# Query, key and value sums of a decoder layer, taken two 128-token blocks at a time

## The chip, the core and the metric

The kernel runs on one core of a Trainium2 chip. A core has five engines with a queue each, and every queue works strictly in its own order: TensorE (PE in the profile; its weight loads are PEld), VectorE (DVE), ScalarE (ACT), GpSimd (POOL) and SyncE (SP), which here only issues DMA transfers. Engines wait for each other by semaphores. Matmul results land in PSUM, which this kernel divides into eight buffers of 128 x 512 float32.

The metric is the device time of one execution in microseconds (us), the median of several runs. A profiled execution gives the trace from which all rows below come; its span runs from the first to the last instruction.

## The reference, cut to what matters

The program is a two-layer decoder trunk on 512 tokens of width 1024. Layer 0 is a convolution module, layer 1 is causal differential attention; each is followed by a gated feed-forward network and a gated per-layer embedding. The change lies in layer 1:

```
u = rms_norm(h, g)                              # 512 x 1024
q, k, v = split(u @ w_qkv, 3)                   # 8 heads, 2 components of 64, v 128 wide
q = rms_norm(q, q_g) / 8;  k = rms_norm(k, k_g) # over each 64
for every block of 128 queries:
    logits = q_blk @ k.T + bias[bucket(distance)], masked to the past
    probs = softmax(logits)
    w = probs[component 0] - lam * probs[component 1]
    out = w @ v
h = h + (rms_norm(out, sub_g) * (1 - lambda_init)) @ w_o
```

Only `u @ w_qkv`, and the order in which parts of the block loop are put between its matmuls, are touched.

## The kernel before, in words

All products are in a split form: a float32 operand is held as a rounded part and its remainder (`hi`, `lo`), and one product is three matmuls (`mm3`, lines 154 to 156): hi by lo, lo by hi, hi by hi. A weight block of 128 x 1024 is loaded by SP into one of two `wraw` buffers, rounded by ACT (line 148), and its remainder is taken by DVE or, for chosen ones, by POOL (line 149); four such pairs can be held.

The activations `u` have the tokens along the free dimension, 8 row blocks of 128 features by 512 tokens. The six slabs of `w_qkv` (`QKV`, line 81) are each four weight blocks, that is eight row blocks of 128 x 512. A "q" slab holds the queries and keys of two heads (a pair), a "v" slab the values of four heads. For each slab and each of four token blocks `tokens` (line 634) sums over the eight row blocks: 24 matmuls of 128 x 128 by 128 x 512 into one buffer of the PSUM tag `mm`, which has four. So a slab is 96 matmuls, and the stage is 576.

What comes after a sum depends on the slab. `values` (650) scales and splits it into the tile `B` (ACT line 654, DVE line 655). `unit` (661) copies it (ACT 670), squares it (ACT 673), sums the squares (DVE 677), takes the power -1/2 on POOL (213) and scales it on POOL (680). `unit_end` (683) comes later: four transposes on TensorE (686) into one of two `tp` buffers, then ACT writes the rounded queries and keys (694, 695), POOL copies the keys to the other half (699), and DVE writes the four remainders (702, 704).

The attention of a head and a block of 128 queries is cut in three steps. `stage_s` makes the scores (TensorE 731, 732, into one of two `sc` buffers), adds the bias and finds the maximum on DVE (734), takes the exponential on ACT (738) and combines the two components on DVE (741 to 743). `stage_t` transposes the result (751), and ACT and DVE split it (753, 754). `stage_a` multiplies it with the values (767, 768); every second block ends with a read by ACT and DVE (774, 775), and the fourth block of a head with its norm (779 to 789). `stage_o` transposes a finished head (796) and splits it (168, 169) for the output product.

The steps stand in one list (line 803 on). The place n of a score step is 4 x head + block; the transpose of the same block stands at n + 2 and the product at n + 3, so from n = 3 to n = 31 there are three steps to every n. The loop over `QKV` (815) hands them out: `take(3 * pace)` gives each token block so many steps, and one is issued after each row block's three matmuls. The last place is for the `unit_end` of the block before. What is left after the six slabs is handed out between the matmuls of the per-layer embedding projection (844 on, three steps per output block) and of the output product (`linear`, 867).

The program's text does not fix the order on the engines: a planner with a model of the engines' times reorders the instructions within their dependencies, and its result is the order that is built. Each engine then keeps to that order.

## Time and profile before

| | us |
|---|---|
| median of 3 runs | 1321.56 |
| lowest and highest run | 1321.38, 1324.51 |
| the profiled execution | 1322.03 |
| its span | 1320.2 |
| TensorE busy | 1283.0 |
| DVE busy | 755.1 |
| ACT busy | 526.1 |
| POOL busy | 258.4 |

The stage of the six slabs lies between 652.3 and 816.5 us of the span, what is left of the attention runs to about 881 us beside the projection and the first output columns. A row of a group gives the line, the engine, the operation, the tiles (output, then inputs, without buffer numbers), the shapes and the count; behind the bar the busy time in us, the mean duration of one in ns, and the idle time of the engine ahead of them with what ended it. A row of the waits gives who waited for whom, the total in us, how often, and the longest. A row of the timeline gives the start, the duration, the engine and the line.

### The profile page before, as it was taken

What the parts mean: (1) busy time and instruction counts of PE and PEld (TensorE: products, weight loads), DVE (VectorE), ACT (ScalarE), POOL (GpSimd) and SP (SyncE); (2) the same over time, 40 slices, a digit from 0 to 9 for tenths busy, and PEclk for the clock granted to TensorE, in tenths of its full rate; (3) what the DMA queues carried; (4) which work ended last, traced back from release to release, by engine and by line L of the source; (5) the groups of instructions that cost most, each with busy time, mean ns of one, the idle gap of its engine ahead of it and who ended that gap; (6) DMA issues with size and microseconds to landing.
All of it is one profiled execution on the core that took longest, in us unless ns stands there. A gap on an engine that the chain in (4) does not pass through costs nothing. (4 is left out here: it accounts for less than half of the span.)

```text
span 1320.2 us, 15336 instructions
## 1 busy us (share of the span) xinstructions
PE 1283.0 (97%) x5852; PEld 1049.5 (79%) x5852; DVE 755.1 (57%) x1168; ACT 526.1 (40%) x830; POOL 258.4 (20%) x208
## 2 busy tenths in 40 slices
PE   8999889999999999999999998899999999999998
PEld 6777658888888888888888887778888888888887
DVE  6988684644344434455668887946543344334445
ACT  5644253422122222244466676734322222222342
POOL 5844342100000000022254544222000000000030
PEclk8999889999999999999999999999999999999999
DMA  6354412232322222233212321313223233332231
GB/s 218 110 170 155 132 33 94 82 97 98 104 98 98 97 96 96 80 104 102 87 65 83 102 73 41 103 34 126 96 96 96 96 97 99 102 97 93 76 123 65
DMA packets 45830, 129.21 MB, mean 98 GB/s; under 512 B 5267, under 2 KB 13587, under 8 KB 45756
## 3 DMA queue, kind: packets, MB, share of 16 engines
q1 hardware_dynamic: 39888, 122.70, 27.9%
q10 hardware_dynamic: 5868, 5.53, 1.3%
q8 instruction: 46, 0.75, 0.2%
q14 instruction: 28, 0.23, 0.1%
HBM read 124.52 MB, written 3.69 MB: 97 GB/s over the span
## 5 line engine op out<-in xcount | busy, mean ns | idle before, releaser
L148 ACT CAST whi<-wraw 128x1024 fp32r<-128x1024 f32 (+2 forms) x214 | 218.6, 1026 | 587.9 <-PE mm L156 367.8
L154 PE MATMUL mm<-A,wlo 128*128 128x512 f32 (+1 forms) x1096 | 426.0, 392 | 7.9 <-ACT A L492 3.8
L155 PE MATMUL mm<-A,whi 128*128 128x512 f32 (+1 forms) x1096 | 429.5, 393 | 1.4 <-DVE A L494 0.9
L156 PE MATMUL mm<-A,whi 128*128 128x512 f32 (+1 forms) x1096 | 426.9, 390 | 0.0
L149 DVE TENSOR_TENSOR wlo<-wraw,whi 128x1024 fp32r<-128x1024 f32 (+2 forms) x207 | 255.4, 1237 | 64.0 <-ACT whi L148 63.7
L154 PEld LDWEIGHTS mm<-A,wlo 128*128 128x128 f32 x1096 | 206.9, 189 | 54.7 <-ACT A L492 4.6
L155 PEld LDWEIGHTS mm<-A,whi 128*128 128x128 f32 x1096 | 207.0, 189 | 47.6 <-DVE A L169 3.2
L156 PEld LDWEIGHTS mm<-A,whi 128*128 128x128 f32 x1096 | 207.1, 189 | 43.5 <-issue 1.4
L188 POOL TENSOR_TENSOR acc<-acc,wk 128x512 f32<-128x512 f32 x42 | 68.6, 1632 | 781.8 <-issue 671.2
L155 PE MATMUL mm<-B,whi 128*128 128x512 f32 x352 | 136.9, 389 | 0.0
L156 PE MATMUL mm<-B,whi 128*128 128x512 f32 x352 | 136.9, 389 | 0.0
L154 PE MATMUL mm<-B,wlo 128*128 128x512 f32 x352 | 136.3, 389 | 0.0
L542 DVE TENSOR_TENSOR big<-mm,rb 128x512 f32<-128x512 f32 x44 | 30.4, 691 | 126.2 <-PE mm L156 126.2
L550 DVE TENSOR_TENSOR h<-mm,h 128x512 f32<-128x512 f32 x48 | 33.0, 691 | 120.7 <-PE mm L156 120.7
L540 DVE TENSOR_TENSOR big<-mm,rb 128x512 f32<-128x512 f32 x44 | 30.4, 691 | 99.3 <-PE mm L156 92.9
L154 PEld LDWEIGHTS mm<-B,wlo 128*128 128x128 f32 x352 | 66.1, 188 | 13.8
L156 PEld LDWEIGHTS mm<-B,whi 128*128 128x128 f32 x352 | 66.1, 188 | 13.7
L155 PEld LDWEIGHTS mm<-B,whi 128*128 128x128 f32 x352 | 66.1, 188 | 13.6
L156 PE MATMUL mm<-whi,A 128*128 128x512 f32 x192 | 75.7, 395 | 0.0
L155 PE MATMUL mm<-wlo,A 128*128 128x512 f32 x192 | 75.0, 396 | 0.0
L154 PE MATMUL mm<-whi,A 128*128 128x512 f32 x192 | 74.8, 396 | 0.0
L213 POOL TENSOR_TENSOR r<-v,mhalf 128x8 f32<-128x8 f32 (+1 forms) x31 | 47.5, 1532 | 121.7 <-DVE v L211 99.2
(193 smaller groups left out, 1426.1 us busy)
## 6 DMA issues: line engine op xcount, KB each, us to landing
wraw<-in_wts SPq DMA_DIRECT2D x194, 512.0 KB, 3.5
D<-in_diag SPq DMA_DIRECT2D x36, 192.0 KB, 3.9
wraw<-in_wts SPq DMA_DIRECT2D x16, 384.0 KB, 2.9
h<-in_xT SPq DMA_DIRECT2D x8, 256.0 KB, 5.3
bias<-scr ACTq DMA_DIRECT2D x8, 256.0 KB, 3.2
out_t<-h SPq DMA_DIRECT2D x7, 256.0 KB, 2.0
wraw<-in_wts SPq DMA_DIRECT2D x4, 256.0 KB, 3.4
wraw<-in_pT SPq DMA_DIRECT2D x4, 256.0 KB, 3.3
```

The source lines that it names most:

```text
L148: A.copy(hi[:, cut], raw[:, cut])
L149: eng.tensor_tensor(lo[:, cut], raw[:, cut], f(hi[:, cut]), ALU.subtract)
L154: T.matmul(acc, al, bh, start=first, stop=False)
L155: T.matmul(acc, ah, bl, start=False, stop=False)
L156: return T.matmul(acc, ah, bh, start=False, stop=last)
L188: self.eng.tensor_tensor(self.acc, self.acc, sq, ALU.add)
L213: last_pow[0] = G.tensor_tensor(r[:, :n], v[:, :n], mhalf[:, :n], ALU.pow)
L540: V.tensor_tensor(tg, pg, rb, ALU.mult)
L542: V.tensor_tensor(tu, pu, rb, ALU.mult)
L550: V.tensor_tensor(h[m], acc, h[m], ALU.add)
```

## The change

A slab's token blocks are now taken in two pairs. `tokens` opens two `mm` buffers and goes through the row blocks once for both, the second block one row block behind the first: three matmuls of the first block with row block n, then three of the second block with row block n - 1. After each such triple one place is free for a step, so a pair has 16 places.

`QKV` now carries two numbers per slab, one for each pair: `take(n)` hands out all steps whose place in the list is below that number. The last number is 21. The `unit_end` of the two blocks of the pair before stand at the 12th and the 14th of the 16 places (12 places are filled with steps or left empty, and the two are set in behind the 11th and at the end); those of the last pair follow behind the stage. `values` and `unit` get the finished sums and run one after the other at the end of a pair.

```diff
-QKV = (("q", 0, (0, 0, 0, 0)), ("v", 0, (0, 1, 1, 0)), ("q", 1, (1, 1, 2, 2)), ("q", 2, (0, 1, 2, 0)), ("v", 1, (1, 2, 2, 2)), ("q", 3, (0, 2, 0, 1)))
+QKV = (("q", 0, (0, 0)), ("v", 0, (2, 4)), ("q", 1, (6, 8)), ("q", 2, (9, 11)), ("v", 1, (14, 17)), ("q", 3, (19, 21)))
...
-    def tokens(ws, tb, between=()):
-        acc = mm()
-        for k in range(NC):
-            a = tuple(t[:, tb * P : (tb + 1) * P] for t in u[k])
-            mm3(acc, a, ws[k], k == 0, k == NC - 1)
-            if k < len(between) and between[k]:
-                between[k]()
+    def tokens(ws, tbs, between):
+
+        accs = [mm() for _ in tbs]
+        for n in range(NC + 1):
+            for acc, tb, k in ((accs[0], tbs[0], n), (accs[1], tbs[1], n - 1)):
+                if 0 <= k < NC:
+                    a = tuple(t[:, tb * P : (tb + 1) * P] for t in u[k])
+                    mm3(acc, a, ws[k], k == 0, k == NC - 1)
+                    if between:
+                        s = between.pop(0)
+                        if s:
+                            s()
...
     def take(n):
-        got, stages[:n] = [s for _, s in stages[:n]], []
+        got = [s for at, s in stages if at < n]
+        del stages[: len(got)]
         return got
 
-    waiting = None
+    waiting = []
     for what, at, pace in QKV:
         ws = slab(GLO if at > 0 else 0)
-        for tb in range(4):
-            between = take(3 * pace[tb])
-            between += [None] * (6 - len(between))
-            if waiting:
-                between.append(partial(unit_end, *waiting))
-                waiting = None
-            if what == "v":
-                values(at, ws, tb, between)
-            else:
-                waiting = unit(at, ws, tb, between)
-    unit_end(*waiting)
+        for i in range(2):
+            between = take(pace[i])
+            between += [None] * (2 * NC - 4 - len(between))
+            for w in waiting:
+                between.insert(len(between) - 1 if w is waiting[0] else len(between), partial(unit_end, *w))
+            waiting = []
+            tbs = 2 * i, 2 * i + 1
+            for tb, (acc, r) in zip(tbs, tokens(ws, tbs, between)):
+                if what == "v":
+                    values(at, tb, acc, r)
+                else:
+                    waiting.append(unit(at, tb, acc, r))
+    for w in waiting:
+        unit_end(*w)
```

More of the change, by code (lines that the diff above doesn't have):

```diff
@@ L644, in tokens, with values @@
             rcol[0] = r
-        return acc, rcol[0][:, tb : tb + 1]
+        return [(acc, rcol[0][:, tb : tb + 1]) for acc, tb in zip(accs, tbs)]
     val = {}
-    def values(s, ws, tb, between):
-        acc, r = tokens(ws, tb, between)
+    def values(s, tb, acc, r):
         vt_ = sb([P, 4, 2, P], f"B{4 * s + tb}", 1, F32R)
@@ L659, in trunk, with unit @@
     qk = {}
-    def unit(pair, ws, tb, between):
+    def unit(pair, tb, acc, r):
         if tb == 0:
@@ L667, in unit @@
                 G.memset(f(qk[pair][4 + c][HALVES[1 - c]]), 0.0)
-        acc, r = tokens(ws, tb, between)
         q = big()
```

## The prediction

> **What bounds the kernel now.** I read the page's busy shares first, then TensorE's waits between 640 and 900 us, then sums by stretch. Columns of the stretches: length, then busy time (count) of PE, PEld, DVE, ACT and POOL, then the granted clock, the DMA share and GB/s.

> ```profile
> PE 1283.0 (97%) x5852; PEld 1049.5 (79%) x5852; DVE 755.1 (57%) x1168; ACT 526.1 (40%) x830; POOL 258.4 (20%) x208
> ```

> ```profile
> PE sc L731 <- DVE st L734: 5.7, 4, 1.7
> PE sc L731 <- DVE st L742: 2.8, 1, 2.8
> PE mm L154 <- DVE wlo L149: 1.7, 1, 1.7
> ```

> ```profile
> 652.30:816.50 164.20, 162.02 (x840) 137.07 (x840) 126.21 (x327) 106.40 (x240) 78.39 (x75) 1.00 0.22 73
> ```

> ```profile
> 816.50:829.40 12.90, 6.38 (x34) 5.19 (x33) 12.58 (x34) 10.37 (x25) 4.92 (x6) 0.80 0.29 103
> 829.40:842.50 13.10, 11.15 (x56) 8.31 (x55) 12.22 (x32) 10.45 (x25) 3.96 (x4) 0.93 0.49 161
> 842.50:861.70 19.20, 19.20 (x118) 17.02 (x117) 17.26 (x54) 15.31 (x40) 2.05 (x2) 1.00 0.18 56
> 861.70:881.40 19.70, 19.49 (x104) 16.50 (x103) 7.18 (x21) 4.04 (x8) 4.10 (x4) 1.00 0.00 1
> ```

> TensorE is busy 97% of the span. The stage that is changed, the query, key and value sums (652.3 to 816.5), has TensorE idle for 164.20 - 162.02 = 2.2 us in all: that is all a better order inside the sums can win. No wait there is for a weight (the one on L149, 1.7 us, comes later). The idle time lies just behind the sums: 12.90 - 6.38 = 6.5 us and then 13.10 - 11.15 = 1.95 us, while DVE is busy 12.58 of 12.90 and 12.22 of 13.10. In this tail DVE is the limit; the waits of the score matmuls (L731) on DVE say the same. From 842.5 on TensorE is full again, since projections and the output product give it work that needs no DVE.

> **The change, part by part.**

> *Order of the matmuls.* All 576 matmuls of the sums stay. Their pitch is 0.23 us:

> ```profile
> 808.01 0.39 PE L154 MATMUL mm<-whi,A 128*128 128x512 f32 x1
> 808.24 0.39 PE L155 MATMUL mm<-wlo,A 128*128 128x512 f32 x1
> ```

> ```profile
> 672.23 0.40 PE L156 MATMUL mm<-whi,A 128*128 128x512 f32 x1
> 672.47 0.40 PE L155 MATMUL mm<-wlo,A 128*128 128x512 f32 x1
> ```

> The rows at 672 show an L155 behind an L156: the planner of the kernel before already mixes two sums here, at the same pitch. A weight row block is now used for six matmuls running instead of three, so weights are due half as fast. As no weight wait is there to be removed, I take 0 for this; between the ends, a gain of the 2.2 us and a loss that the third rival prices, it is nearest to 0.

> *Two banks per pair.* The `mm` tag has four buffers. A pair holds two, an open attention product one or two. The second sum of the next pair can start when the first sum of the last pair has been read, which takes two ACT passes (rows below, 0.69 us each). Where the planner expects a bank late, the built order has up to 18 matmuls of the first sum ahead, 4 us of cover. I take 0; uncovered, 1.4 us of reading less the three matmuls (0.7) by which the second sum starts later would cost 0.7 us at each of 11 boundaries, 7.6 us.

> *Unit ends per pair.* Squares, the power and the scaling of two blocks now come at once, and their transposes are placed behind the 12th and 14th of the next pair's 16 triples, 12 x 3 x 0.23 = 8.3 and 9.7 us on.

> ```profile
> L670 ACT ACTIVATE big<-mm,rcol 128x512 f32<-128x512 f32 x16 | 11.0, 690 | 10.0 <-DVE rcol L643 5.5 <-PE mm L156 4.3
> L673 ACT ACTIVATE wk<-mm,rcol 128x512 f32<-128x512 f32 x16 | 11.0, 688 | 0.0
> ```

> ```profile
> L213 POOL TENSOR_TENSOR r<-v,mhalf 128x8 f32<-128x8 f32 x16 | 28.5, 1778 | 33.0 <-ACT wth L753 13.9 <-DVE v L211 12.3 <-DVE st L742 4.9
> L680 POOL TENSOR_TENSOR big<-big,r 128x512 f32<-128x512 f32 x16 | 16.8, 1049 | 1.2
> ...
> L149 POOL TENSOR_TENSOR wlo<-wraw,whi 128x1024 fp32r<-128x1024 f32 x4 | 9.6, 2398 | 9.1 <-issue 9.1
> ```

> Two units need 4 x 0.69 on ACT and 2 x (1.78 + 1.05) on POOL, with a short reduction on DVE between: the first is ready after some 5.6, the second after 8.4 us, so both are just covered. If POOL's weight split (2.40) falls in between, one wait of about 1.8 us per slab follows, four slabs, 7 us at most. I take 0.

> *The handing out.* This is the part with a price. The old pace hands out 21 x 3 = 63 steps between the sums; the new one hands out all steps with n below 21, which is 3 x 20 - 2 = 58. Five steps move behind the sums: scores of head 5 blocks 1 and 2 (256 and 384 wide), transposes of head 4 block 3 (512) and head 5 block 0 (128), and the product of head 4 block 2. None of them issues a DMA (a head's bias load belongs to its block 0, and those of heads 6 and 7 stay behind the sums).

> ```profile
> L149 DVE TENSOR_TENSOR wlo<-wraw,whi 128x1024 fp32r<-128x1024 f32 x22 | 28.7, 1310 | 3.9 <-ACT whi L148 3.8
> L704 DVE SCALAR_TENSOR_TENSOR C<-tp,vec,C 64x256 fp32r<-64x256 f32 x32 | 15.5, 484 | 0.6
> ...
> L677 DVE TENSOR_REDUCE v<-wk 128x8 f32<-128x512 f32 x16 | 10.9, 682 | 5.7 <-ACT wk L673 5.5
> ...
> L734 DVE CUSTOM_DVE_ANT_0 big<-sc,bias 128x512 f32<-128x512 f32 x8 | 5.5, 683 | 0.0
> L754 DVE TENSOR_TENSOR wtl<-tp,wth 128x512 fp32r<-128x512 f32 x8 | 5.5, 682 | 0.2
> ...
> L743 DVE SCALAR_TENSOR_TENSOR big<-acc,st,big 128x384 f32<-128x384 f32 x8 | 4.9, 616 | 0.2
> L743 DVE SCALAR_TENSOR_TENSOR big<-rb,st,big 128x256 f32<-128x256 f32 x8 | 4.6, 575 | 0.2
> L734 DVE CUSTOM_DVE_ANT_0 big<-sc,bias 128x384 f32<-128x384 f32 x8 | 4.4, 551 | 0.4 <-PE sc L732 0.3
> ...
> L734 DVE CUSTOM_DVE_ANT_0 rb<-sc,bias 128x256 f32<-128x256 f32 x8 | 3.3, 418 | 2.3 <-PE sc L732 2.2
> ```

> ```profile
> 816.49 0.28 PE L767 MATMUL mm<-B,wth 128*128 128x256 f32 x1
> ...
> 817.36 0.45 PE L731 MATMUL sc<-C,C 128*128 128x512 f32 x1
> ```

> On DVE the moved steps cost 2 x 0.42 + 0.58 (256), 2 x 0.55 + 0.62 (384), 0.68 and some 0.3 (the two transposes), and about 1.0 of one-column work: 5.1 us. Besides, the ends of units bunch: of the last slab one more block's four splits (4 x 0.48 = 1.9) and one more L677 (0.7) lie behind the last sum. DVE gets 7.7 us more in the tail. On TensorE the moved steps take about 2.3 us (four pairs of the product take 817.36 - 816.49 = 0.87, so three 0.65; scores and transposes about 1.65, an estimate from their widths at that pitch). So the sums end 2.3 us earlier and the tail is 2.3 us longer; that alone is 0.

> Now the tail in the built order. Ahead of the first projection matmul DVE has 12 splits (5.8), two L677 (1.4), scores 2 x 0.42 + 2 x 0.55 + 0.68 (2.6), one 256 combination (0.6), a 512-wide split (0.7), the first projection weight (1.3) and about 1.2 of small work: 13.6 us after the sums, against 12.9 now (816.5 to 829.4). That is +0.7.

> Then TensorE has 18 projection matmuls, three pairs, a score and two transposed heads, some 5.8 us, and waits for a transpose bank. DVE frees it after a 512 score (0.7), a split (0.7), the last block's four (1.9), two combinations (0.6 and 0.7), three weight splits (3.9), two head splits (512 wide, 0.7 each) and small work: 11 us, and the weight loads add to that. The buffer of projection weight 2 is freed only by the split of weight 1, so its load begins there:

> ```profile
> wraw<-in_wts SPq DMA_DIRECT2D x194, 512.0 KB, 3.5
> ```

> ```profile
> 826.43 1.04 ACT L148 CAST whi<-wraw 128x1024 fp32r<-128x1024 f32 x1 [1.96 <-DMA wraw<-in_wts]
> ```

> With 3.5 us of landing ahead of its cast, and the fourth weight one split and one landing later, I put DVE's extra wait at 2 us: 13 us, of which TensorE idles 7.2, against 1.95 now: +5.2. Next late is the 384 score of head 6, whose bank DVE frees about 2 us after TensorE comes to it: +2. From this goes what the slow clock costs today:

> ```profile
> 823.00:826.00 3.00, 0.44 (x2) 0.30 (x2) 2.89 (x10) 1.48 (x5) 2.92 (x2) 0.72 0.83 283
> 826.00:829.00 3.00, 1.93 (x8) 1.86 (x9) 2.97 (x10) 2.44 (x5) 0.02 (x1) 0.50 0.34 135
> 829.00:832.00 3.00, 3.00 (x13) 2.56 (x12) 2.94 (x10) 2.78 (x7) 1.83 (x3) 0.64 0.57 194
> ```

> At 0.50 and 0.64 some 2 us of TensorE's work in the last two rows is the clock's. The dip returns, but in front of a wait for DVE, which hides it: -2. The sum is 0.7 + 5.2 + 2 - 2 = 5.9 us; DVE's durations overlap by some hundredths each, so I take 5.5.

> The clock fell to 0.50 here with no single wait over 2.8 us. [...]

> The sum stands against the profiled execution: 1320.2 us of span in 1322.03 us, 0.5 us over the median of 1321.56. 1322.0 + 5.5 - 0.5 = **1327 us**.

> **Rivals.**

> *The tail's idle time swallows the moved steps (faster).* If the 8.5 us of idle time there is latency of a chain and not DVE's load, the moved 2.3 us of TensorE work fits in free, and with the 2.2 us inside the sums gone the time is 1321.6 - 4.5 = 1317. It decides if DVE is idle for more than 7.7 us between 816.5 and 861.7; the rows give 45.2 - 42.1 = 3.1. Chance 0.10.

> *Nothing to see.* DVE is busy only 7.18 of the last 19.70 us, and TensorE's other work there can be done while heads 6 and 7 are late; and the planner mixed sums before, so the order may be no real change. Then 1321 to 1324. Against it: the built order puts the late waits ahead of that work. Chance 0.25.

> *Waits inside the sums.* Banks (7.6) or POOL (7) as priced above, half of it, on top of the forecast: about 1334. Only 2.2 us of such waits now speaks against it. Chance 0.13.

> *Alternating banks slows TensorE.* If changing the sum every three matmuls made small gaps that drop the clock in a tenth of the stage, 0.1 x 576 x 0.23 = 13 us more, 1335. The rows at 672 alternate at full pitch, and the stage has clock 1.00. Chance 0.02. [...]

> **How the numbers follow.** The forecast keeps 0.50. Run to run, 0.3% (4 us, 1317.6 to 1325.5) is what can be told from no change. Of the forecast, 0.05 falls below that, so slower is 0.45 + 0.13 + 0.02 = 0.60, same 0.25 + 0.05 = 0.30, faster 0.10. The range leaves out the faster rival and the far ends of the third: 1318 to 1334. Alone, the forecast spans 1323 (half of DVE's 7.7 us hidden) to 1330 (all of it bare, and the sums no shorter).

> **What would show it.** Right: the sums end about 2 us earlier with clock 1.00 and no more than 4 us idle in them; behind them TensorE idles 15 us or more over the next 30 us with DVE above 90%, and one wait of over 4 us for a tile that DVE reads (L169's line). Wrong: waits on ACT or POOL at the pair boundaries, a weight wait in the sums, or a tail as long as today's.

## The result and the profile after

The changed kernel took 1329.75 us (median of 6 runs, 1328.71 to 1331.03), the kernel before, beside it on the same chip, 1322.74 us (6 runs, 1321.38 to 1324.89). The ratio is 1.0051, with a 95% interval of 1.0038 to 1.0064: slower by about 7 us. The profiled execution of the changed kernel took 1328.71 us with a span of 1326.9 us, against 1322.03 and 1320.2 us before.

In the changed kernel, line numbers are higher by one up to about L634 and by four behind it: L735 is the score matmul (L731 before), L738 its reduction, L755 the transposes of attention weights, L170 the split of a transposed head, L150 the split of a weight, L690 a unit end's transposes, L706 and L708 its splits. First the engines' busy line on the page, then the stretches of the changed kernel with the columns that the prediction explains.

```profile
PE 1288.5 (97%) x5852; PEld 1053.2 (79%) x5852; DVE 755.9 (57%) x1168; ACT 525.6 (40%) x830; POOL 252.4 (19%) x208
```

```profile
652.30:812.80 160.50, 159.44 (x818) 134.00 (x817) 121.35 (x309) 100.87 (x227) 72.32 (x72) 1.00 0.24 75
812.80:826.40 13.60, 8.14 (x31) 4.94 (x29) 12.33 (x33) 10.28 (x24) 7.59 (x9) 0.69 0.14 39
826.40:839.20 12.80, 8.54 (x34) 7.07 (x34) 10.00 (x18) 8.76 (x16) 0.81 (x2) 0.77 0.57 186
839.20:848.40 9.20, 9.19 (x42) 8.28 (x43) 6.38 (x22) 6.84 (x18) 1.01 (x1) 0.67 0.17 58
848.40:868.00 19.60, 19.60 (x121) 17.45 (x119) 15.01 (x53) 12.64 (x34) 3.09 (x3) 1.00 0.15 55
```

TensorE has the same 5852 instructions and is busy 1288.5 us instead of 1283.0. The sums end 3.7 us earlier than before (812.8 instead of 816.5) and TensorE is idle in them for 160.50 - 159.44 = 1.1 us instead of 2.2. What is lost is lost behind them. The granted clock stands at 0.69, 0.77 and 0.67 over three stretches, where the kernel before had 0.80, 0.93 and then 1.00.

From 640 us to the end, the kernel before and then the changed one:

```profile
640.00:1320.20 680.20, 662.48 (x3126) 550.89 (x3124) 391.84 (x726) 289.86 (x514) 123.06 (x108) 0.99 0.27 88
```

```profile
640.00:1326.90 686.90, 668.30 (x3128) 554.66 (x3126) 392.77 (x727) 289.84 (x515) 117.15 (x108) 0.98 0.27 87
```

Of the 6.7 us, 5.8 (668.30 - 662.48) are TensorE being busy longer with the same matmuls, and only 0.9 (18.6 instead of 17.7) are more idle time. The next rows are the stretches with the halved clock behind the sums, before and then after:

```profile
824.30:831.20 6.90, 4.13 (x15) 3.74 (x15) 6.76 (x20) 4.76 (x11) 2.67 (x5) 0.51 0.52 187
```

```profile
817.90:831.60 13.70, 10.65 (x33) 7.57 (x32) 12.50 (x32) 9.68 (x21) 6.22 (x9) 0.50 0.39 116
838.30:845.30 7.00, 6.08 (x26) 5.65 (x27) 5.40 (x17) 4.51 (x15) 0.00 (x0) 0.51 0.22 75
```

At half clock a matmul of 512 columns follows the one before it in 0.43 us instead of 0.23 (in the changed kernel 827.03 to 827.46, against 832.57 to 832.80), so by estimate about half of TensorE's busy time there is the clock's: 4.13 / 2 = 2.1 us before, (10.65 + 6.08) / 2 = 8.4 us after. That is 6.3 us more, nearly the whole difference. It doesn't follow that the clock alone is the cause: in the long stretch DVE is busy 12.50 of 13.70 us, so a faster TensorE would mostly have waited for DVE there. In the second one DVE is busy 5.40 of 7.00, and TensorE 6.08: there up to 3 us of the clock can lie on the path.

What stands ahead of that second stretch shows in the waits of TensorE from 640 to 900 us, and in the rows of TensorE, ACT and DVE:

```profile
PE tp L755 <- DVE A L170: 4.2, 1, 4.2
PE sc L735 <- DVE st L738: 3.4, 4, 1.1
PE mm L155 <- DVE wlo L150: 2.1, 2, 1.8
...
PE tp L690 <- POOL big L684: 1.1, 1, 1.1
```

```profile
826.44 0.79 PE L155 MATMUL mm<-C,wlo 128*128 128x512 f32 x1 [0.37 <-DVE wlo L150]
...
839.22 1.12 PE L755 MATMUL tp<-ident,big 128*128 128x128 f32 x4 [4.23 <-DVE A L170]
```

```profile
833.10 1.05 ACT L149 CAST whi<-wraw 128x1024 fp32r<-128x1024 f32 x1 [2.18 <-DMA wraw<-in_wts]
836.20 1.04 ACT L149 CAST whi<-wraw 128x1024 fp32r<-128x1024 f32 x1 [1.47 <-DMA wraw<-in_wts]
```

```profile
837.27 1.23 DVE L150 TENSOR_TENSOR wlo<-wraw,whi 128x1024 fp32r<-128x1024 f32 x1 [1.86 <-ACT whi L149]
```

TensorE waits 4.23 us for a transpose bank, which DVE frees when it has split a transposed head (L170). Ahead of that split DVE stands for 1.86 us, because a weight comes late. The clock falls within that wait.

### The profile page after: what moved, and what is told of

Read it like the earlier page. It is cut to its first block, busy times and chain, and to the rows that moved or that the text cites. A ratio compares the mean times of both kernels' runs of the same rounds, so it can differ in the third digit from the quotient of the medians.

```text
span 1326.9 us, 15343 instructions
## 1 busy us (share of the span) xinstructions
PE 1288.5 (97%) x5852; PEld 1053.2 (79%) x5852; DVE 755.9 (57%) x1168; ACT 525.6 (40%) x830; POOL 252.4 (19%) x208
## 4 chain that ended last, share of the span: by engine, by line
PE 84%; DVE 6%; ACT 2%; DMA 2%; POOL 1%; issue 1%; ACTq 0%; POOLq 0%; DVEq 0%
PE mm L155 26%; PE mm L156 26%; PE mm L157 26%; DVE sc L373 2%; POOL wk L365 1%; DVE wlo L150 1%; PE mm L301 1%; PE mm L771 1%; PE mm L328 1%; PE tp L755 1%; PE sc L736 1%; ACT whi L149 1%; PE sc L735 1%; DMA wraw<-in_wts 1%; DMA po<-big 0%
## 5 line engine op out<-in xcount | busy, mean ns | idle before, releaser
L149 ACT CAST whi<-wraw 128x1024 fp32r<-128x1024 f32 (+2 forms) x214 | 218.7, 1026 | 592.3 <-PE mm L157 375.8
L155 PE MATMUL mm<-A,wlo 128*128 128x512 f32 (+1 forms) x1096 | 425.9, 392 | 8.3 <-ACT A L493 3.8
L156 PE MATMUL mm<-A,whi 128*128 128x512 f32 (+1 forms) x1096 | 429.6, 393 | 1.2 <-DVE A L495 0.9
L150 DVE TENSOR_TENSOR wlo<-wraw,whi 128x1024 fp32r<-128x1024 f32 (+2 forms) x207 | 254.1, 1230 | 68.4 <-ACT whi L149 67.8
L155 PEld LDWEIGHTS mm<-A,wlo 128*128 128x128 f32 x1096 | 206.8, 189 | 55.0 <-ACT A L493 4.6
L156 PEld LDWEIGHTS mm<-A,whi 128*128 128x128 f32 x1096 | 207.1, 189 | 47.6 <-DVE A L170 3.0
L156 PE MATMUL mm<-B,whi 128*128 128x512 f32 x352 | 137.0, 389 | 0.0
L155 PE MATMUL mm<-B,wlo 128*128 128x512 f32 x352 | 136.3, 389 | 0.0
L156 PEld LDWEIGHTS mm<-B,whi 128*128 128x128 f32 x352 | 66.1, 188 | 13.8
L155 PEld LDWEIGHTS mm<-B,wlo 128*128 128x128 f32 x352 | 66.1, 188 | 13.7
L157 PEld LDWEIGHTS mm<-B,whi 128*128 128x128 f32 x352 | 66.1, 188 | 13.6
L155 PE MATMUL mm<-whi,A 128*128 128x512 f32 x192 | 76.3, 399 | 0.0
L156 PE MATMUL mm<-wlo,A 128*128 128x512 f32 x192 | 75.6, 396 | 0.0
L365 POOL TENSOR_TENSOR wk<-wk,C 128x512 f32<-128x512 f32 x43 | 65.0, 1514 | 28.7 <-ACT C L364 26.0
## 6 DMA issues: line engine op xcount, KB each, us to landing
wraw<-in_wts SPq DMA_DIRECT2D x194, 512.0 KB, 3.5
```

Of the source, the lines that this page charges most:

```text
L149: A.copy(hi[:, cut], raw[:, cut])
L150: eng.tensor_tensor(lo[:, cut], raw[:, cut], f(hi[:, cut]), ALU.subtract)
L155: T.matmul(acc, al, bh, start=first, stop=False)
L156: T.matmul(acc, ah, bl, start=False, stop=False)
L157: return T.matmul(acc, ah, bh, start=False, stop=last)
L365: G.tensor_tensor(pacc, pacc, pr, ALU.add)
```

## The experiments

The theory at the start was the prediction's: steps of attention that no longer lie between the sums, and DVE's work for them, make the part behind the sums longer. The rivals: the pairing itself (its banks, its unit ends) costs, or only the clock differs. The table collects all runs. "Steps" is how many are handed out between the sums; "sums end" is the end of the last sum's matmul in the profiled execution, and "behind" is the span less that.

| kernel | steps | sums end | behind | median us | ratio to before (95%) |
|---|---|---|---|---|---|
| before | 63 | 816.7 | 503.6 | 1322.7 to 1323.6 | 1 |
| changed | 58 | 813.0 | 513.9 | 1329.75 | 1.0051 (1.0038 to 1.0064) |
| b57: before, fewer steps | 57 | 813.6 | 513.7 | 1329.15 | 1.0053 (1.0039 to 1.0067) |
| b66: before, more steps | 66 | 818.3 | 507.6 | 1327.49 | 1.0032 (1.0019 to 1.0044) |
| a64: changed, more steps | 64 | 816.6 | 516.4 | 1335.19 | 1.0091 (1.0077 to 1.0105) |
| a67: changed, still more | 67 | 823.8 | 511.2 | 1336.58 | 1.0094 (1.0080 to 1.0108) |
| aseq: pair's sums in turn | 58 | 814.9 | 515.2 | 1332.42 | 1.0071 (1.0058 to 1.0083) |
| alast58: last pair single | 58 | 814.2 | 512.0 | 1328.03 | 1.0035 (1.0021 to 1.0048) |
| alast63: the same | 63 | 821.2 | 506.6 | 1328.45 | 1.0037 (1.0025 to 1.0050) |
| araw: changed, early weights | 58 | 813.8 | 511.4 | 1329.41 | 1.0038 (1.0026 to 1.0051) |
| braw: before, early weights | 63 | 816.8 | 509.3 | 1329.41 | 1.0042 (1.0030 to 1.0055) |
| apool: changed, splits on POOL | 58 | 813.5 | 511.0 | 1329.91 | 1.0047 (1.0034 to 1.0059) |
| bpool: before, splits on POOL | 63 | 818.3 | 508.5 | 1328.02 | 1.0035 (1.0023 to 1.0048) |
| afill: changed, filler matmuls | 58 | 813.6 | 513.9 | 1329.41 | 1.0049 (1.0035 to 1.0063) |

The profiled executions of apool (1326.32 us) and araw (1326.98) are the fastest of their kernels, 3.6 and 2.4 us below the medians; their traces show the good end of the spread.

**b57: fewer steps in the old order.**

```diff
-... ("q", 3, (0, 2, 0, 1)))
+... ("q", 3, (0, 1, 0, 0)))
```

> The kernel before, one block at a time, but with 57 steps handed out instead of 63 (the last slab's blocks get 0, 3, 0, 0 steps): the new hand-out's count without the pairing. Theory 1: slower by 4 to 8 us, 1326 to 1330, with a wait of over 3 us of TensorE for a transpose bank that DVE frees between 830 and 850 us, and a second slow-clock stretch behind it. Theory 2 (the pairing itself is the loss): within 2 us of the kernel before, 1320 to 1324.

Measured: 1329.15 us, the changed kernel's loss without any pairing. Its last sum, its waits from 640 to 900 us and its two stretches at half clock:

```profile
813.22 0.40 PE L156 MATMUL mm<-whi,A 128*128 128x512 f32 x1
```

```profile
PE sc L731 <- DVE st L734: 9.3, 6, 2.5
PE tp L686 <- DVE C L704: 1.8, 1, 1.8
```

```profile
820.70:834.40 13.70, 9.24 (x28) 6.65 (x29) 13.39 (x31) 9.24 (x19) 2.50 (x5) 0.50 0.38 128
841.10:844.60 3.50, 3.50 (x17) 3.17 (x17) 2.35 (x11) 2.13 (x9) 0.00 (x0) 0.51 0.81 239
```

Against the last sum of the kernel before,

```profile
816.26 0.39 PE L156 MATMUL mm<-whi,A 128*128 128x512 f32 x1
```

the sums end 3.0 us earlier and what is behind them takes 10.1 us longer (513.7 - 503.6). The changed kernel has the same two numbers: 3.7 and 10.3. Averaged over the six, a step costs 3.0 / 6 = 0.5 us among the sums and 10.1 / 6 = 1.7 us behind them, with the waits and the slow clock that come with it. Too few steps among the sums is enough to make the whole loss, and it makes it in the same place: DVE 13.39 of 13.70 us busy, and a second stretch at half clock that begins a little after 840. One detail was missed: no wait of over 3 us is needed. The longest is 2.5 us, and the scores' waits come to 9.3 us in six pieces instead.

**a64 and a67: the steps given back to the pairs.** In a64 the last pair takes steps with n below 23 instead of 21; in a67 the last three limits are 18, 21 and 24.

```diff
-... ("v", 1, (14, 17)), ("q", 3, (19, 21)))
+... ("v", 1, (14, 17)), ("q", 3, (19, 23)))     # a64
+... ("v", 1, (14, 18)), ("q", 3, (21, 24)))     # a67
```

> The changed kernel, but the last pair of blocks is handed all steps with n below 23 instead of 21: 3 x 22 - 2 = 64 steps lie between the sums, one more than before, instead of 58. Theory 1 (the six steps behind the sums, and DVE's work for them, are the loss): the sums end about 2.5 us later than in the changed kernel (815.3 instead of 812.8), the wait of 4.2 us for the transpose bank shrinks to 2 us or less, the second stretch of slow clock behind it goes, and the time falls by about 5 us to 1321 to 1325. Theory 2 (the loss is in the pairing itself, its banks and its unit ends): the time stays at 1328 to 1331. Theory 3 (only the length of the first slow-clock stretch behind the sums differs): the time stays within 2 us of 1329.7, with 3 us or more at 0.50 there again.

> The changed kernel with still more handed out: n below 18 in the last pair of the second values, below 21 and 24 in the last two pairs: 3 x 23 - 2 = 67 steps between the sums, four more than before. Theory 1 (moved steps and DVE's load in the tail): the sums end about 1.5 us later than in the kernel before, the tail is shorter by more, TensorE never waits over 3 us behind the first projection matmul; 1316 to 1322, faster than before or equal. Theory 2 (the pairing itself): 1328 or more, since nothing of the pairing is undone. A middle outcome, 1322 to 1326, would say that DVE inside the last sums is loaded to the point where steps put there come late.

Measured: 1335.19 and 1336.58 us, some 5 to 7 us slower than the changed kernel. Theory 1 has the sign wrong in both, and no theory gives the 1335 of a64; a67 lies within theory 2's "1328 or more", and what is left of that theory is the late unit ends. In TensorE's rows of a64 (the first three) and of a67 a different wait has come:

```profile
821.56 0.30 PE L735 MATMUL sc<-C,C 128*128 128x128 f32 x1 [1.84 <-DVE C L706]
826.11 0.55 PE L735 MATMUL sc<-C,C 128*128 128x256 f32 x1 [3.81 <-DVE C L706]
...
841.91 0.66 PE L690 MATMUL tp<-ident,big 128*128 128x128 f32 x4 [1.84 <-POOL big L684]
```

```profile
829.34 0.55 PE L735 MATMUL sc<-C,C 128*128 128x256 f32 x1 [1.65 <-POOL C L703]
```

With 64 steps gone, one score block of head 5 is left behind the sums; the next scores, 128 and 256 wide, are head 6's. Head 6 needs the queries and keys of the last slab, and the unit ends of that slab's first pair stand only in the last pair's sums, behind its 12th and 14th triple, so their splits (C, L706) run when the sums are over. The scores wait for them, 1.84 + 3.81 us, the first projection matmul then waits 3.67 us for the split of its weight, and the last unit end's four transposes start at 841.91. In the kernel before the last four start at 827.85:

```profile
827.85 1.06 PE L686 MATMUL tp<-ident,big 128*128 128x128 f32 x4
```

In the changed kernel the last four start at 823.12: by these rows the steps of head 5 that it leaves behind the sums are what covers the chain. So the theory was half right: the count is a price, and it has a price on its other side as well. In a67 something else adds to it: its sums end 7.1 us later than before. They hold four steps more, and inside them, between 780 and 800 us, TensorE is idle for 1.9 us and then at half clock for 3.4:

```profile
780.00:800.00 20.00, 18.12 (x85) 14.77 (x85) 18.54 (x52) 12.68 (x30) 5.35 (x4) 0.91 0.29 92
```

**b66: the other side in the old order.**

```diff
-... ("q", 3, (0, 2, 0, 1)))
+... ("q", 3, (0, 2, 1, 1)))
```

> The kernel before, one block at a time, with 66 steps handed out instead of 63 (three more, in block 2 of the last slab). The kernel of before with 57 steps was 5.9 us slower: its sums ended 3.0 us earlier and what lies behind them took 10.1 us longer, 1.7 us for a step behind the sums against 0.5 for one among them. If every step behind the sums costs that (the count decides), three more among them gain about 3.5 us: 1318 to 1321, faster than both kernels. If the steps of head 5 that are left behind the sums cover the unit ends on which head 6 waits (as the changed kernel with 64 and 67 steps suggests, 5 to 7 us slower than with 58), there is a best number and it is near 63: 1325 to 1332, with TensorE waiting 2 us or more for the splits of the unit ends ahead of the first projection matmul.

Measured: 1327.49 us, slower, as the second reading said. TensorE's rows:

```profile
822.40 0.36 PE L731 MATMUL sc<-C,C 128*128 128x256 f32 x1 [0.75 <-DVE C L702]
...
833.52 0.66 PE L686 MATMUL tp<-ident,big 128*128 128x128 f32 x4 [1.02 <-POOL big L680]
...
837.42 0.47 PE L731 MATMUL sc<-C,C 128*128 128x512 f32 x1 [1.26 <-DVE C L702]
```

The scores again wait for a unit end's splits, here C from L702, and the last unit end comes at 833.5 instead of 827.9. The waits are smaller than the 2 us that were expected; three stretches at half clock (6.8 us from 824.6, 3.4 from 838.2 and 3.4 from 845.0, together some 11.6 us of busy TensorE) take up to 5.8 us. With 57, 63 and 66 steps the old order takes 1329, 1323 and 1327 us: the best number of the three is the one it had.

**aseq: the pair's two sums one after the other.**

```diff
-        for n in range(NC + 1):
-            for acc, tb, k in ((accs[0], tbs[0], n), (accs[1], tbs[1], n - 1)):
-                if 0 <= k < NC:
+        for acc, tb in zip(accs, tbs):
+            for k in range(NC):
+                if True:
```

> The changed kernel, with the same hand-out and the same unit ends per pair, but the two sums of a pair one after the other instead of interleaved row block by row block. Theory 1 (what counts is how many steps lie behind the sums): within 2 us of the changed kernel, 1328 to 1332. Theory 2 (the interleaving and its two open banks cost time): back towards the time before, 1322 to 1326.

Measured: 1332.42 us, a ratio of 1.0071 against the changed kernel's 1.0051, with intervals that overlap a little (1.0058 to 1.0064). So interleaving shows no cost; if anything it saves some. Without it TensorE waits 5.03 us for a unit end that POOL scales, ahead of this row:

```profile
826.07 1.12 PE L690 MATMUL tp<-ident,big 128*128 128x128 f32 x4 [5.03 <-POOL big L684]
```

**alast58 and alast63: only the last pair one block at a time.** The unit ends of the last slab's first pair are put into the sum of block 2 and the start of block 3's, block 2's own into block 3's sum. In alast63 one of the steps taken is dropped by the edit: it leaves out the product of head 4's block 3, with the scaling of that head. The lines are those of alast58; alast63 also raises the limits of the pairs ahead (15, 19 and 22) and hands out two steps in block 3's sum.

```diff
+            if (what, at, i) == ("q", 3, 1):
+                break
...
+    ends = [partial(unit_end, *w) for w in waiting]
+    between = take(21) + [None, ends[0]]                                   # alast58
+    u2 = unit(3, 2, *tokens(ws, (2,), between)[0])
+    between = [None, ends[1]] + [None] * 4 + [partial(unit_end, *u2)]
+    waiting = [unit(3, 3, *tokens(ws, (3,), between)[0])]
```

> The changed kernel, but the last pair of blocks (2 and 3 of the last slab) is summed one block at a time, and the steps are handed out so that 63 lie between the sums, at about the places of the kernel before; the other eleven pairs stay pairs. Theory 4 (formed after the first four runs: the loss is in how the last pair ends, with two unit ends and few steps of attention bunched behind the last sum; elsewhere the pairs cost nothing and save a little): back to the time before or just below, 1319 to 1323. Rival (pairs anywhere in the stage cost, by later unit ends or banks): 1326 or more.

> As alast63, the last two blocks one at a time, but with the changed kernel's 58 steps handed out. Together with alast63 it separates the number of steps from the last pair's two unit ends. If the number of steps decides (as the kernel of before with 57 steps suggests, 6 us slower): 1326 to 1331, like the changed kernel. If the two unit ends at once decide: 1320 to 1324.

Measured: 1328.45 and 1328.03 us, both slower than before by 0.35%. Theory 4 falls: taking the last pair apart gives back about 2 us (1.0035 against 1.0051, intervals overlapping), with 58 steps and with 63. alast63, with the hand-out of the kernel before, has a part behind the sums (506.6) that is 7 us shorter than the changed kernel's, and loses that in the sums, which end at 821.2, 4.5 us later than before. In its sums, too, TensorE is idle between 780 and 800 us, 2.3 us, with a fall of the clock behind it, where the kernel before has none:

```profile
780.00:800.00 20.00, 17.71 (x88) 14.77 (x87) 16.97 (x47) 11.99 (x30) 6.69 (x6) 0.91 0.28 92
```

Since it leaves work out, it only bounds what a full kernel of that kind would do.

**araw and braw: no wait for the two raw buffers.** The two projection weights go, in halves, into tiles of the input that the sums no longer need.

```diff
-            w = weight()
+            w = weight(halves=("A12", "A13") if m == 0 else ("A14", "A15"))
```

> The changed kernel, but the two projection weights that follow the sums are loaded into buffers of the input that the sums have just finished with, each in two halves of 512 columns, so that they and the output weights behind them no longer wait for one of the two raw buffers; one more cast and one more split per weight, about 1 us of DVE. Theory 5 (the 4.2 us wait and the slow clock behind it come from DVE and ACT idling for late weights, 2.18 and 1.47 us on ACT and 1.86 us on DVE): the wait falls below 2.5 us, the clock stretch at 839 to 847 goes, 1323 to 1326. If the moved work of DVE alone is the cause: 1329 to 1332, since DVE only gets more to do.

> The kernel before with the same change of the weight buffers, as the control for araw: here DVE is busy over 90% through the first 45 us behind the sums and doesn't wait for those weights for more than 0.74 us, so no gain: 1321 to 1325. If it gains as much as araw does, late weights are a cost of both kernels and not what the change added.

Measured: 1329.41 us for both. In araw's profiled execution the long wait shrank as expected (line numbers are six higher there: L761 is the transposes, L176 the head's split):

```profile
PE tp L761 <- DVE A L176: 2.3, 1, 2.3
```

The time hardly followed: the medians differ by 0.3 us, the ratios by 0.0013 with intervals that overlap. The mechanism of the wait was right, its worth wasn't. And the control, with earlier weights, was 5.8 us slower than the kernel before: there the first projection matmul comes at 823.5 instead of 829.4 and a 384-wide score at 832.5 instead of 827.1, so projections went ahead of scores, and the rest of the order moved.

**apool and bpool: three splits moved from DVE to POOL.** The splits of the second projection weight and of the first two output weights run on POOL.

```diff
-            w = weight()
+            w = weight(eng=G if m == 4 else V)
...
-    linear(NC, ot, add_attn, 2, heads_until, step)
+    linear(NC, ot, add_attn, 2, heads_until, step, first=2)
```

> The changed kernel, but three weight splits of the tail (the second projection weight and the first two output weights, 1.31 us each on DVE) run on POOL, which is busy under a fifth of that time; 3.9 us less for DVE behind the sums, TensorE's order as in the changed kernel up to the long wait. If DVE's load behind the sums is what the change pays for: the 4.2 us wait falls by 2.5 to 4 us, the slow-clock stretch behind it goes too, and the time is 1322 to 1326. If the order of the tail and the clock's windows decide, whatever DVE has to do: 1328 or more.

> The same three splits moved to POOL in the kernel before, as the control. If DVE's load bounds that tail too: 1317 to 1321, about 3 us faster than before, and the idle 1.95 us in the second stretch behind the sums goes. If the tail of before is as short as its other chains allow, and any new order is worse (as moving the weight buffers was, +5.5 us): 1324 to 1330.

Measured: 1329.91 and 1328.02 us. In apool the wait halves and the second slow stretch shrinks from 7.0 to 3.4 us, in its fastest execution:

```profile
PE tp L755 <- DVE A L170: 2.1, 1, 2.1
```

```profile
838.20:841.60 3.40, 3.32 (x16) 2.92 (x15) 2.22 (x9) 2.90 (x9) 2.38 (x1) 0.54 0.53 154
```

Over five runs nothing is gained, and bpool loses 5 us against the kernel before. But the edit did not take 3.9 us off DVE. Small instructions of DVE lasted longer in bpool, the first of them until a split on POOL ended (833.04 and 833.02 us); these are POOL's and DVE's rows:

```profile
830.65 2.37 POOL L149 TENSOR_TENSOR wlo<-wraw,whi 128x1024 fp32r<-128x1024 f32 x1 [2.99 <-ACT whi L148]
```

```profile
831.04 2.00 DVE L211 TENSOR_SCALAR v<-v 128x4 f32<-128x4 f32 x1
836.25 1.52 DVE L787 TENSOR_TENSOR r<-r,r 128x4 f32<-128x4 f32 x1
839.57 1.65 DVE L742 SCALAR_TENSOR_TENSOR st<-st,lam 128x1 f32<-128x1 f32 x1
```

The same three took 0.17, 0.15 and 0.22 us in the kernel before, so 4.6 us came back. From 816 to 885 us DVE is busy 51.29 us in the kernel before and 52.04 in bpool:

```profile
816.00:885.00 69.00, 59.54 (x320) 49.57 (x319) 51.29 (x141) 42.15 (x97) 15.11 (x16) 0.95 0.20 66
```

```profile
816.00:885.00 69.00, 58.89 (x304) 49.39 (x303) 52.04 (x137) 42.78 (x99) 20.53 (x20) 0.88 0.21 66
```

In apool one instruction of one column took 2.15 us, and DVE is busy 50.11 us there against 51.06 in the changed kernel. So these two runs don't tell what a lighter DVE would be worth.

**afill: TensorE kept busy.** 36 matmuls that nobody reads, 12, 16 and 8 ahead of the first three projections, placed among the scores.

```diff
+        for _ in range({0: 12, 1: 16, 2: 8}.get(m, 0) if val else 0):
+            T.matmul(acc[:, : 2 * P], ones_r, val[0, 0], start=True, stop=True)
```

> The changed kernel with 36 extra matmuls of 256 columns (0.12 us each, 4.1 us together) that write a bank ahead of its own first matmul and so change no result; they stand in three lots among the scores behind the sums, where TensorE idles for DVE. If the slow clock is what costs the 7 us (by the trace TensorE does 8.3 us less than it could in the slow stretches, 2.1 before): the stretch at 817 to 832 goes or halves, and the time falls to 1323 to 1327. If the slow clock there only fills time in which TensorE would wait for DVE anyway: 1329 to 1334.

Measured: 1329.41 us. The first slow stretch starts seven us later and the second is half as long:

```profile
824.90:835.10 10.20, 7.24 (x23) 5.17 (x23) 9.97 (x20) 7.23 (x15) 1.55 (x4) 0.50 0.53 177
841.90:845.40 3.50, 3.50 (x18) 3.40 (x16) 2.44 (x9) 2.65 (x8) 0.00 (x0) 0.51 0.39 139
```

The clock's share falls from 8.4 to 5.4 us, the filler adds some 4.4 us of work (36 matmuls at about 0.12, from 814.15 to 815.59, 816.63 to 817.82 and 818.06 to 819.88), and the end doesn't move. In the first stretch the slow clock fills time in which DVE (9.97 of 10.20) would mostly be waited for anyway. The granted clock over the whole execution says the same: it is 0.987 on average over the five runs of afill and over the 37 of the kernel before that the experiments have beside them, and 0.984 in the changed kernel. With the clock of the one, afill has the time of the other, so the clock alone isn't the loss; how much of it the filler's own work hides, no run shows.

No kernel of these beats the one before; all twelve are 0.3 to 0.9% slower than it.

## Why the prediction was right or wrong

The direction and the size were right (1327 against 1329.75, within the range), and that moved steps are enough for such a loss is shown by b57. The bookkeeping of the tail was partly wrong. It adds 0.7 + 5.2 + 2 = 7.9 us of idle time and takes off 2 us of slow clock; measured from 640 us on, idle time grew by 0.9 us and the clock's share by 6.3.

*Order of the matmuls, 0.* Idle time in the sums fell from 2.2 to 1.1 us, at clock 1.00. That is a gain of 1.1 where none was counted, and aseq points the same way.

*Two banks per pair and unit ends per pair, 0 each.* Right within the sums: no wait for a read bank shows, and the one wait of 1.1 us for POOL lies behind the sums. But the step looked only at who waits in the sums. The later unit ends cost what a64 and a67 show: they take away the freedom to hand out more.

*The handing out.* The sums were to end 2.3 us earlier and ended 3.7 earlier, of which the 2.3 and the 1.1 of idle time make 3.4. The first projection matmul was to come 13.6 us behind the sums, and came 826.4 - 812.8 = 13.6 behind.

*The wait for the transpose bank, +5.2.* It was there, on the line named, and it was mis-sized: 4.23 us instead of 7.2, so 2.3 more idle than before instead of 5.2. DVE's side of it was right: it freed the bank 839.2 - 826.4 = 12.8 us behind the first projection matmul, against 13. But TensorE, at half clock until 831.6, was busy for 8.5 of them instead of 5.8.

*The 384 score's bank, +2.* Not there: from 839.2 to 848.4 TensorE is idle for 0.01 us.

*The slow clock, -2.* This is the step that failed. The first stretch didn't go; it doubled, from 6.9 to 13.7 us, with DVE busy for 12.5 of them. And a second one of 7.0 us, for which the forecast has no term, began within the 4.2 us wait and lasted beyond it, with TensorE busy for 6.08 of it. That the clock fell in the kernel before without a wait over 2.8 us was no argument against a fall behind a long wait: in the changed kernel it fell at 817.9 behind waits of 1.1 us at most and at 838.4 within one of 4.23. So the place of the loss and the points that DVE sets (13.6 and 12.8 us) were foreseen, the kind of loss was not: slow clock stood where idle time was counted, and that the two nearly cancelled, 5.5 against 7, was luck.

*Rivals.* "The tail swallows the steps" falls with b57, which is 5.9 us slower with six steps more there. "Nothing to see" falls with the interval. "Waits inside the sums" falls with 1.1 us of idle time there, and "alternating banks" with the clock of 1.00.

*What would show it.* TensorE was to be idle 15 us or more over 30 us with DVE above 90%. It is idle 5.5 + 4.3 us in the first 26, and DVE is at 91% and then 78%: the slow clock stands where idle time was expected. The other signs came: the earlier end of the sums, their clock of 1.00, and one wait of 4.2 us on the line named.

What stays open: how the 10 us behind the sums divide among DVE's work, the waits and the clock. A wait (araw) and the clock's share (afill) were made smaller, and neither gave back time that five runs can tell; DVE's work was hardly made smaller by apool. Each of these edits also reorders what follows, so a single suspect was never changed quite alone. In the profiled executions half clock stands for 6.8 us between 780 and 880 us in the kernel before, for 20.5 us in the changed one and for some 13.7 to 24 us in b57, b66, a64, a67, aseq, apool and afill, all of them slower; whether it makes them slower or only goes with their idle time, that doesn't say. A hand-out for pairs that is as good as the old one wasn't found; one with full work, singles at the end and 61 to 63 steps wasn't tried.

## What to carry to other kernels

Work that is handed out between long sums had a best amount here: with less, the engine behind the sums gets a bunch of small dependent steps, in b57 at 1.7 us each instead of 0.5, and with more, nothing is left to cover the chain that ends the sums. When a change regroups the sums, count both: the steps left behind them, and which of them do not depend on the sums' own last results. Read a stretch by granted clock and busy time together; a total of idle time that hardly changes (0.9 us here) can hide a loss of 6 us in busy time (668.30 instead of 662.48). And price the whole stretch: a wait shortened in one place (4.2 to 2.1 us) was worth nothing over five runs. Where work is moved to another engine, look at the time that was gained on the engine it was taken from before reading the result: in bpool three small instructions of DVE took 5.17 us instead of 0.54.

## What was not expected of the hardware

The clock didn't need a long wait to fall: in the changed kernel no wait of TensorE from 800 us to its first fall at 817.9 is over 1.1 us. The next four rows are 3.4 us each just ahead of a fall in the changed kernel (twice), in b57 and in b66:

```profile
814.50:817.90 3.40, 1.44 (x5) 0.89 (x6) 3.23 (x11) 3.35 (x10) 1.89 (x2) 1.00 0.00 0
834.90:838.30 3.40, 0.08 (x1) 0.00 (x0) 1.54 (x2) 2.10 (x4) 0.00 (x0) 1.00 0.63 220
```

```profile
837.70:841.10 3.40, 1.45 (x12) 1.12 (x11) 2.97 (x5) 3.40 (x7) 0.00 (x0) 1.00 0.24 59
```

```profile
841.60:845.00 3.40, 1.92 (x12) 1.36 (x13) 2.98 (x7) 3.09 (x7) 0.00 (x0) 1.00 0.00 0
```

and this one, in the kernel before, is followed by full clock:

```profile
817.50:820.90 3.40, 1.73 (x10) 1.04 (x8) 3.28 (x9) 3.03 (x8) 0.30 (x1) 1.00 0.00 0
```
